# Conditioning as fp32 matmuls on raw weight tiles, and query/key splits placed behind their transposes, in a two-layer hybrid attention/Fourier step

## The chip, the cores and the metric

The kernel runs on one core of a Trainium2 chip. The metric is the device time of one execution in microseconds. Before the change three runs took 1280.7, 1283.64 and 1284.29 us (median 1283.64).

The core has five engines with an instruction queue of their own: TensorE (PE in the profile, its weight loads PEld), VectorE (DVE), ScalarE (ACT), GpSimd (POOL) and SyncE (SP), which here only issues transfers. Each works through its queue in order; semaphores tie the queues together.

## What is computed

Two layers of a backbone with 1024 features, for 1024 latent tokens and 256 context tokens (ten tiles of 128 tokens, tiles 8 and 9 context). All values are fp32. Cut to what matters here:

```python
def ada_mod(cvec, w, b):
    m = jax.nn.silu(cvec) @ w + b            # w: 1024 x 3072
    return jnp.split(m, 3, axis=-1)          # shift, scale, gate

for l in range(2):
    shc, scc, gtc = ada_mod(c_ctx, ada_w[l], ada_b[l])     # context tokens
    shl, scl, gtl = ada_mod(c, ada_w[l], ada_b[l])         # latent tokens
    hc = modulate(rms_norm(xc, norm_g[l]), shc, scc)       # h * (1 + scale) + shift
    hl = modulate(rms_norm(xl, norm_g[l]), shl, scl)
    yc, yl = mixer(l, hc, hl)      # l=0: attention A and B, gated; l=1: Fourier mixing, gated
    xc, xl = xc + gtc * yc, xl + gtl * yl

# attention A: 8 query heads, 2 key/value heads of width 64
qa = rope(rms_norm(qa, gq)); ka = rope(rms_norm(ka, gk))
p = softmax((qa * 64 ** -0.5) @ concat(ka, ka_ctx).T); oa = p @ concat(va, va_ctx)
# attention B: window of +-128 tokens plus all context keys, and a sink logit per head
```

The conditioning is thus a product of two vectors (c and c_ctx) with two matrices of 1024 x 3072: six parts of 4 MB, named (layer, part) with part 0 the shift, 1 the scale, 2 the gate. Each part is read in eight tiles of 512 KB.

## The kernel before

**Precision.** TensorE multiplies fp32r operands in one pass. To get near fp32, a value is split into a high half (rounded to fp32r) and a low half (the rest), by `copy` for the high half (L261 on ACT, L263 on DVE) and a subtract for the low one (L267 or L641). A product of two such values then takes three matmuls.

**The order of the work.** The program is written in the order of its stages, and a scheduler turns that into one order for each engine. SBUF is cut by hand into pools of equal buffers (`ZONES`: 26 `u`, 8 `w`, 2 `q`, 3 `pt`, 4 `p`, 9 `h`, 4 `e`); `take` gives the longest-free buffer among the pools named, in program order, so a transfer into a buffer waits until its last reader is done. PSUM's banks are three rings: `s` and `t` of three, `a` and `g` of one.

**Opening.** Over eight chunks k of 128 features, `ada_chunk` computes shift and scale of layer 0 for that chunk and the projections of the first tokens follow. A raw tile (128x8x128: eight blocks of 128 rows, 128 columns) is split into halves, and multiplied with `cs4` (the SiLU of the two vectors in both halves, four columns) as the stationary operand: eight matmuls for the high half (L491, four result rows), eight for the low half (L493, two). The rows go to SBUF (L496), and a matmul with `comb` (L499) adds the halves and turns the result into columns, from which `modb` and `moda` are made (L503, L504).

**S1.** A list of steps (`S1`) written by hand: cached keys (`c`), statistics and modulation of the second and third token groups (`n`, `m`), and keys and queries of attention A (`k`, `q`, `K`, `Q`). Each projection returns a function `post`, its finishing; `Filler.run` holds it back until `depth` later steps have been issued (1 in S1). In `q_pair` and `kv_pair` the projected, normalised and rotated queries and keys are split into halves of 128x256 each (`split_v`: `copy` L263 and L641), side by side as `[hi lo]`; `post` transposes the 128-column pieces as fp32r (`transp`, L646), evicts them (`kev`, `qev`) and stores queries to DRAM in `qd` (L762). Before a block of scores `load_q` reads them back (L845) into the `q` pool.

**Attention A.** For each key/value head, ten query tiles (`soft` and the `sL`, `sC` scores at L840, transposes of the probabilities L957, the products with values L963). Between these, work of a `Filler` is pumped in by cost: the remaining projections, by the names in `ORDER` (qa1, kb0, qb0, qb1, f1, g0, ...). With three of them (`COND` = qb0, qb1, g0) go the parts (0, 2), (1, 0) and (1, 1) of the conditioning, by the class `Rows`: in `step_ap` each of the eight tiles (128 rows x 1024) is loaded on SP (L348), multiplied and added to an accumulator for the first vector by two DVE instructions (L351), scaled for the second on ACT (L355) and added on POOL (L356). `finish` then sums the accumulators over the 128 partitions by matmuls with `ones2` (L365, eight of 512 columns, after a split), and turns the rows into columns by eight transposes (`row_to_mod`, L309) or, for a gate, stores them to DRAM in `gtd`.

**Layer 1.** The last part (1, 2), `r2`, stands in the stage of the gate projection (`g1E`, `g1O`, `g1c`, in four chunks): `Rows.step` with four DVE instructions a tile (L339), spread over the last three chunks, and `finish` behind the fourth. Behind that come row sums (L1427, L1429) for the Fourier mixer's first matmuls (`u`).

Of the kernel before, what the change touches and what calls it, by code (L numbers as in the profile page):

```python
# [17 lines left out]
P = 128  # L18
# [12 lines left out]
S1 = "c1 n2 m1 c0 m2 K0 Q0 Q2 K2 k6 q8 k4 k8".split()  # L31
E_ML = ("p", "d")
E_MF, E_MH, LC0 = "da", "d", "ppd"
E_AH, E_AL = "a", "dpp"
# [11 lines left out]
FC, XF = 1.3, False  # L46
AT_C, WO1 = (1, 1), ((0, 1, 2, 3), (), (4,), (5, 6), (7,))
# [4 lines left out]
COND = ("qb0", "qb1", "g0")  # L52
# [70 lines left out]
def hybrid_step(ctx: ExitStack, tc: tile.TileContext, I, O):  # L123
# [44 lines left out]
    qd = dr.tile([NT, 4, 2, 64, 512], F32, name="qd")  # L168
# [26 lines left out]
    cs4 = cp.tile([P, 8, 4], F32R, name="cs4")  # L195
    comb = cp.tile([4, 2], F32, name="comb")
    bT1 = cp.tile([P, 8], F32, name="bT1")
    gT = cp.tile([P, 2, 8], F32, name="gT")
    bT = cp.tile([P, 2, 16], F32, name="bT")
# [17 lines left out]
    dve.tensor_copy(cs4[:, :, 0:2], cs)  # L217
    dve.tensor_sub(cs4[:, :, 2:4], cs, cs4[:, :, 0:2])
    dve.tensor_add(comb, ident[0:4, 0:2], ident[0:4, 2:4])
# [86 lines left out]
    def row_to_mod(l, part, row):  # L306
        tp = t_bank(f"modt{l}{part}")
        for k in range(8):
            pe.transpose(tp[:, 2 * k : 2 * k + 2], row[0:2, k * P : k * P + P], ident[0:2, 0:2])  # L309
        tv = tp[:, 0:16].rearrange("p (k v) -> p k v", v=2)  # L310
# [3 lines left out]
        else:  # L314
# [4 lines left out]
    def ada_src(l, part, k):  # L319
        return I["ada_w"][l, k * P : (k + 1) * P, part * D : (part + 1) * D]  # L320

    class Rows:
        def __init__(self, l, part, name, tags):
            self.l, self.part, self.name, self.tags = l, part, name, tags
            self.acc = [take(tags, (P, D)) for v in range(2)]
            for a in self.acc:
                pool.memset(a.a, 0.0)
                if part == 2:
                    sp.dma_start(a[0:1, :], I["ada_b"][l : l + 1, 2 * D : 3 * D])

        def step(self, k, wt=None):
            own = wt is None
            if own:
                wt = take(self.tags, (P, D))
                sp.dma_start(wt.a, ada_src(self.l, self.part, k))
            for v in range(2):
                for h in range(2):
                    sl = slice(h * 512, h * 512 + 512)
                    dve.scalar_tensor_tensor(  # L339
# [1489 lines left out]
```

## Time and profile before

| what | value |
|---|---|
| runs | 1280.7, 1283.64, 1284.29 us (median 1283.64) |
| the profiled execution's own time | 1282.65 us |
| its span (first to last instruction) | 1280.9 us |
| mean granted TensorE clock | 0.971 |
| busy: PE, DVE, ACT, POOL | 1191.8, 955.5, 639.3, 489.1 us |
| opening | 0 to about 88 us |
| S1 up to the first scores | 88 to 141 us |
| attention A | 141 to about 560 us |
| gate projection of layer 1 | about 1000 to 1075 us |

How to read the quoted lines. A line of a group reads: line of the kernel, engine, operation, result <- operands, tile sizes, count | busy us, mean ns of one | idle time of that engine just ahead of them and what ended it. A line of the waits: the waiting engine, line and tile <- what ended the wait: total us, times, longest us. A line of the chain or the timeline begins with its start and its length in us; the length of a group of matmuls runs to the end of its last one, and ends are modelled, so the distance between two starts is the better price. A matmul on fp32 operands leaves two records (the 16 `comb` matmuls leave 32).

### The profile page before, as it was taken

To read this page: it belongs to the slowest core of one execution; us is meant where nothing else is said; L and a number is where in the kernel's file an instruction comes from. 1 tells how busy PE (TensorE), PEld (TensorE's weight loads), DVE (VectorE), ACT (ScalarE), POOL (GpSimd) and SP (SyncE) were. 2 spreads that over 40 slices of the span, in tenths; PEclk is the share of its full clock that TensorE was granted. 3 is DMA by queue.
4 is the path that set the end of the run, shared out by engine and by line. 5 is a ranking of instruction groups with operands and counts; after the bars stand their busy time and mean duration, and the time that the engine had idled before them with its cause. 6 is when DMAs were issued, how large, how long until landed. Compare 5 with 4: busy or idle time off the path is not lost.

```text
span 1280.9 us, 21997 instructions
## 1 busy us (share of the span) xinstructions
PE 1191.8 (93%) x7883; PEld 1066.0 (83%) x7883; DVE 955.5 (75%) x2114; ACT 639.3 (50%) x1239; POOL 489.1 (38%) x386
## 2 busy tenths in 40 slices
PE   5789899999889899999999978889999998999997
PEld 5788899999879798889999977767777888988886
DVE  6789788776987987977887867466874988548553
ACT  5363366565675576756655677431264324333221
POOL 6757665522775754530101042310411215335001
PEclk8898899999999999999999989889999999999999
DMA  9900332324634336344433388596412544346321
GB/s 303 290 6 31 110 90 71 98 68 107 188 110 134 103 122 177 112 138 129 105 90 87 95 241 223 135 253 202 138 59 75 158 154 142 101 140 191 124 90 66
DMA packets 156199, 168.29 MB, mean 131 GB/s; under 512 B 21917, under 2 KB 117161, under 8 KB 156090
## 3 DMA queue, kind: packets, MB, share of 16 engines
q1 hardware_dynamic: 156090, 166.89, 44.4%
q8 instruction: 62, 1.02, 0.4%
q14 instruction: 47, 0.39, 0.1%
HBM read 122.67 MB, written 44.18 MB: 130 GB/s over the span
## 4 chain that ended last, share of the span: by engine, by line
PE 62%; DVE 15%; DMA 11%; issue 5%; POOL 4%; ACT 3%; SPq 1%; POOLq 0%; DVEq 0%; ACTq 0%
PE ga L249 7%; PE of L249 7%; PE av L963 7%; PE pt L957 6%; PE oz L249 5%; PE q L249 4%; PE u L249 4%; PE g1E L249 4%; PE sL L840 3%; PE g1O L249 2%; DVE w L351 2%; PE kv L249 2%; PE sC L840 2%; DVE p L874 2%; DMA od<-e 2%
## 5 line engine op out<-in xcount | busy, mean ns | idle before, releaser
L960 DVE TENSOR_TENSOR pt<-pt,pt 128x512 fp32r<-128x512 f32 (+1 forms) x264 | 171.1, 658 | 34.5 <-ACT pt L261 34.1
L963 PE MATMUL av<-pt,u 128*128 128x256 f32 x1008 | 171.0, 292 | 7.4 <-DVE pt L960 4.0
L261 ACT ACTIVATE pt<-pt 128x512 fp32r<-128x512 f32 (+1 forms) x264 | 146.9, 574 | 60.8 <-PE pt L957 36.4
L957 PE MATMUL pt<-identr,p 128*128 128x128 f32 x1008 | 156.6, 274 | 0.7 <-ACT h L261 0.5
L963 PEld LDWEIGHTS av<-pt,u 128*128 128x128 f32 x1008 | 142.0, 192 | 16.6 <-DVE pt L960 7.1
L267 POOL TENSOR_TENSOR w<-h,w 128x512 fp32r<-128x512 f32 x58 | 79.6, 1384 | 180.6 <-ACT w L261 78.7
L249 PE MATMUL q<-w,u 128*128 128x256 f32 x864 | 132.3, 294 | 1.8 <-DVE u L438 1.0
L957 PEld LDWEIGHTS pt<-identr,p 128*128 128x128 f32 x1008 | 119.7, 141 | 9.5 <-ACT h L261 0.9
L249 PE MATMUL ga<-u,w 128*128 128x512 f32 (+1 forms) x576 | 123.5, 360 | 0.1
L881 ACT ACTIVATE p<-p,nm 128x1280 f32<-128x1280 f32 (+1 forms) x80 | 95.3, 1192 | 54.7 <-DVE p L874 54.3
L249 PEld LDWEIGHTS q<-w,u 128*128 128x128 f32 x864 | 117.1, 195 | 6.1 <-DVE u L438 1.8
L249 PEld LDWEIGHTS ga<-u,w 128*128 128x128 f32 x576 | 93.7, 188 | 15.0 <-ACT pt L261 0.6
L840 PE MATMUL sL<-u,q 128*128 128x512 f32 x256 | 85.2, 418 | 11.6 <-DVE p L874 8.5
L249 PE MATMUL oz<-u,w 128*128 128x512 f32 x240 | 68.5, 413 | 9.8 <-ACT w L261 9.8
L356 POOL TENSOR_TENSOR w<-w,w 128x1024 f32<-128x1024 f32 x24 | 58.6, 2442 | 43.9 <-ACT w L355 33.4
L881 ACT ACTIVATE p<-p,NM 128x640 f32<-128x640 f32 (+2 forms) x80 | 59.2, 740 | 32.4 <-DVE p L874 32.2
L840 PE MATMUL sC<-u,q 128*128 128x256 f32 x320 | 63.2, 300 | 9.4 <-DMA q<-qd 5.8
L249 PE MATMUL of<-u,u 128*128 128x512 f32 (+1 forms) x219 | 65.8, 388 | 0.0
L249 PEld LDWEIGHTS oz<-u,w 128*128 128x128 f32 x240 | 45.9, 196 | 20.0 <-ACT w L261 10.4
L874 DVE TENSOR_SCALAR_CACHE_REDUCE p<-sC,nsink 128x256 f32<-128x256 f32 x80 | 37.8, 475 | 30.3 <-PE sC L840 25.6
L840 PEld LDWEIGHTS sC<-u,q 128*128 128x128 f32 x320 | 48.9, 192 | 13.4 <-issue 5.8
L249 PE MATMUL kv<-w,u 128*128 128x256 f32 x384 | 56.2, 290 | 0.0
(773 smaller groups left out, 2881.8 us busy)
## 6 DMA issues: line engine op xcount, KB each, us to landing
q<-qd SPq DMA_DIRECT2D x80, 256.0 KB
w<-i_ada_w SPq DMA_DIRECT2D x24, 512.0 KB
h<-i_w_in SPq DMA_DIRECT2D x40, 256.0 KB
qd<-h SPq DMA_DIRECT2D x40, 256.0 KB
h<-i_w_out SPq DMA_DIRECT2D x32, 256.0 KB
h<-i_wuT SPq DMA_DIRECT2D x16, 256.0 KB
u<-i_x SPq DMA_DIRECT2D x8, 512.0 KB
p<-i_ada_w SPq DMA_DIRECT2D x8, 512.0 KB
```

The costliest lines, as they stand in the source:

```text
L249: pe.matmul(out, a, b, start=i == 0, stop=i == n - 1)
L261: act.activation(out, in_, AF.Copy)
L267: pick("lo" + lc, lc).tensor_sub(dst_l, src, dst_h)
L351: dve.scalar_tensor_tensor(out=self.acc[0][:, sl], in0=wt[:, sl], scalar=cs[:, k, 0:1], in1=self.acc[0][:, sl], op0=ALU.mult, op1=ALU.add,)
L356: pool.tensor_add(self.acc[1].a, self.acc[1].a, wt.a)
L840: pe.matmul(ps, q[:, s, hc * P : hc * P + P], keys, start=s == 0, stop=s == 1)
L874: dve.tensor_scalar(p[i][:, end[i] : end[i] + n], ps, sign, last[i], op0=ALU.mult, op1=ALU.min, accum_out=c)
L881: act.activation(p[i][:, 0 : end[i]], p[i][:, 0 : end[i]], AF.Exp, bias=last[i], scale=-1.0, accum_out=SU[:, t, hd + i, 0:1],)
L957: pe.transpose(tp[:, jj * 256 + i * P : jj * 256 + i * P + P], p[i][:, off : off + P], ident)
L960: dve.tensor_sub(pt[:, 1, 0:n], tp[:, 0:n], pt[:, 0, 0:n])
L963: pe.matmul(acc, vv, pt[:, s, jj * 256 : jj * 256 + 256], start=c + jj + s == 0, stop=c + jj == nt - 1 and s == 1,)
```

## The change

**Conditioning.** All 48 tiles of the conditioning are now column tiles (128x8x128) that go to TensorE raw: `ada_mm` takes each 128x128 fp32 block as the stationary operand and `cs` (128x2) as the moving one, eight fp32 matmuls a tile, accumulating straight into columns in PSUM. `cs4`, `comb`, the splits, the class `Rows` and `row_to_mod` are gone. The 16 tiles of (0, 0) and (0, 1) stay in the opening. The other 32 are issued in S1 ahead of its steps, in the numbers of `AT_N` (0, 0, 2, 2, 2, 2, 3, 3, 3, 3, 4, 4, 4), into the pools `p`, `pt`, `q`, with the `a` bank for the sum. The gate parts are transposed once at the end of S1 (`gate_rows`) and stored to `gtd`.

**Queries and keys.** They are transposed unsplit as fp32 (four transposes for a pair of query tiles in place of eight, two for a pair of key tiles in place of four) and split when they are taken from PSUM: a `copy` for the high half, a DVE subtract for the low one. The halves of the keys come to lie in separate partitions (`key_split`; `kd` has the high half in one part and the low in the other, loaded in four pieces). Queries are staged in a 4 KB tile from the pools of `QE_Z` in place of two buffers of `h`, and `qd` and the scores' indexing (`q_at`) follow.

**Finishing.** In S1 `depth` is 3 in place of 1.

```diff
+AT_N, AT_Z = (0, 0, 2, 2, 2, 2, 3, 3, 3, 3, 4, 4, 4), ("p", "pt", "q")
+QE_Z = ("pt", "q", "w", "u", "p")
-COND = ("qb0", "qb1", "g0")
...
+    def ada_mm(out, raw, first, last):
+        for b in range(8):
+            pe.matmul(out, raw[:, b, :], cs[:, b, :], start=first and b == 0, stop=last and b == 7)
+        drop(raw)
...
+    def ada_step(l, part, k, raw, tag="g"):
+        if k == 0:
+            acc_ada[l, part] = bank(tag, f"ada{l}{part}")
+        ps = acc_ada[l, part]
+        ada_mm(ps[:, 2 * k : 2 * k + 2], raw, k == 0, k == 7)
+        if k < 7:
+            return
...
+        else:
+            col = take("e", (P, 2, 8))
+            dve.tensor_add(col.a.rearrange("p v k -> p k v"), tv, bb)
+
+            def row_out():
+                tp = t_bank(f"gt{l}")
+                pe.transpose(tp[0:16, 0:P], col.a.rearrange("p v k -> p (v k)"), ident)
+                row = take("e", (16, P))
+                act.activation(row.a, tp[0:16, 0:P], AF.Copy)
+                sp.dma_start(gtd[l].rearrange("v (k c) -> (v k) c", c=P), row.a)
...
     def ada_chunk(k, raws):
         ps = bank("g", f"ada{k}")
         for part, raw in enumerate(raws):
-            hi, lo = take("u", (P, 8, P), F32R), take("u", (P, 8, P), F32R)
-            split(hi.a, lo.a, raw.a, E_AH, E_AL)
-            drop(raw)
-            out = ps[0:4, part * P : part * P + P]
-            for b in range(8):
-                pe.matmul(out, cs4[:, b, :], hi[:, b, :], start=b == 0, stop=False)
-            for b in range(8):
-                pe.matmul(out[0:2], cs4[:, b, 0:2], lo[:, b, :], start=False, stop=b == 7)
-            drop(hi, lo)
...
+            ada_mm(ps[:, 2 * part : 2 * part + 2], raw, part == 0, part == 1)
...
+    def transp(name, y, n):
+        tp = t_bank(name)
         for i in range(n):
-            pe.transpose(tp[:, i * P : i * P + P], y2[:, i, :], identr)
+            pe.transpose(tp[:, i * P : i * P + P], y[:, i, :], ident)
         return tp
+    def key_split(dst, tp, h):
+        a, b = 64 * h, 64 - 64 * h
+        copy("kev", E_KEV, dst[a : a + 64], tp[a : a + 64])
+        dve.tensor_sub(dst[b : b + 64], tp[a : a + 64], dst[a : a + 64])
...
         def post():
+            tp = transp(f"qT{m}{kv}{t}", y.rearrange("p t (a h) d -> p (t a) (h d)", h=2), 4)
+            tv = tp.rearrange("p (t n) -> p t n", t=2)
+            qe = take(QE_Z, (P, 2, 2, 256), F32R)
+            copy("qev", E_QEV, qe[:, :, 0, :], tv)
+            dve.tensor_sub(qe[:, :, 1, :], tv, qe[:, :, 0, :])
             for i in range(2):
-                tp = transp(f"qT{m}{kv}{t}{i}", y2[i].a, 4)
-                qe = take("h", (P, 512))
-                copy("qev", E_QEV, qe.a, tp)
-                sp.dma_start(qd[t + i, 2 * m + kv].rearrange("a d f -> (a d) f"), qe.a)
+                sp.dma_start(qd[t + i, 2 * m + kv], qe[:, i].rearrange("p a n -> p (a n)").bitcast(F32))
...
     fl_ = Filler()
-    fl_.depth = 1
+    fl_.depth = 3
...
+    todo_ada = deque((l, part, k) for l, part in ((0, 2), (1, 0), (1, 1), (1, 2)) for k in range(8))
+    def ada_fill(n):
+        for _ in range(min(n, len(todo_ada))):
+            l, part, k = todo_ada.popleft()
+            ada_step(l, part, k, ada_tile(l, part, k, AT_Z), "a")
     for n, op in enumerate(S1):
+        ada_fill(AT_N[n])
...
-        if nm in cond:
-            for n in range(4):
-                cost, fn, key = (*work[n], None)[:3]
-                fl_.add(0.5 * cost, fn, key)
-                fl_.add(0.0, cond_steps(cond[nm], (2 * n,)))
-                fl_.add(0.5 * cost, cond_steps(cond[nm], (2 * n + 1,)))
...
-    r2 = Rows(1, 2, "ad12", BIG)
-        for k in ((), (0, 1, 2), (3, 4, 5), (6, 7))[c]:
-            r2.step(k)
-    r2.finish("g")
```

**How the order moves.** In these rows stand a row's number on its engine, the line of the kernel, the operation, the result <- operands by the program's names, and the size with its count.

First TensorE in S1. The change has four blocks of this kind (here the first, at row 360; the others at 387, 408 and 509), in which the eight tiles of one part follow each other; `q` are projections of queries, `kT` a transpose of keys:

```order
359 L244 MATMUL q_1371<-w_376,u_992 128x256
360 L313 MATMUL ada_813<-cs,p_811 128x2 x8
361 L313 MATMUL ada_813<-cs,pt_822 128x2 x8
362 L313 MATMUL ada_813<-cs,q_912 128x2 x8
363 L313 MATMUL ada_813<-cs,p_922 128x2 x8
364 L313 MATMUL ada_813<-cs,pt_942 128x2 x8
365 L313 MATMUL ada_813<-cs,q_952 128x2 x8
366 L313 MATMUL ada_813<-cs,p_1022 128x2 x8
367 L313 MATMUL ada_813<-cs,p_1032 128x2 x8
368 L583 MATMUL kT_1322<-identr,q_1046 128x128 x2
369 L244 MATMUL q_1371<-w_375,u_993 128x256
```

Before, no conditioning stands between the opening and the first scores (`sL`), of which this is the place:

```order
611 L249 MATMUL q_1828<-w_438,u_1110 128x256
612 L249 MATMUL q_1828<-w_439,u_1110 128x256
613 L249 MATMUL q_1828<-w_438,u_1111 128x256
614 L646 MATMUL kT_1686<-identr,p_1562 128x128 x4
615 L840 MATMUL sL_0000_1708<-u_1019,q_1701 128x512 x2
616 L249 MATMUL q_2001<-w_428,u_1050 128x256
```

All four blocks stand ahead of the first scores, which are row 573 in the change; after the last conditioning tile of the opening (row 212) come 77 matmuls of projections before the next transposes of x.

Second SP's queue around that place, in the change: raw tiles (`i_ada_w`) into the pools `p`, `pt` and `q`, stores of queries (`qd<-`), then the first loads of queries (`q<-qd`):

```order
91 L308 DMA q_1457<-i_ada_w 128x8x128
92 L308 DMA pt_1467<-i_ada_w 128x8x128
93 L710 DMA qd<-p_1563 128x512 x2
94 L308 DMA p_1568<-i_ada_w 128x8x128
95 L308 DMA p_1578<-i_ada_w 128x8x128
96 L308 DMA pt_1588<-i_ada_w 128x8x128
97 L807 DMA q_1750<-qd 64x2x512 x2
98 L807 DMA q_1946<-qd 64x2x512 x2
```

Before, the queue holds only the stores, weights and loads there:

```order
65 L762 DMA qd<-h_1414 128x512
66 L282 DMA h_1672<-i_w_in 128x2x256
67 L282 DMA h_1668<-i_w_in 128x2x256
68 L845 DMA q_1701<-qd 64x2x512
69 L704 DMA o_new_v_a<-h_1625 128x128 x2
70 L762 DMA qd<-h_1655 128x512
```

The 32 raw tiles of S1 are rows 59 to 96 of SP's queue; the two loads of queries stand behind all of them. Later, in attention A, the staging tiles of the queries lie in the `q` pool for most pairs, between the loads that use its two buffers.

Third TensorE at the passage from the gate projection (`g1c`) to the Fourier mixer (`u`), before:

```order
5056 L249 MATMUL g1c_12675<-u_11710,u_12261 128x256
5057 L249 MATMUL g1c_12675<-u_11709,w_12262 128x256
5058 L365 MATMUL ad12p_12710<-h_12711,ones_88 2x512
5059 L365 MATMUL ad12p_12710<-h_12712,ones_88 2x512
5060 L365 MATMUL ad12p_12710<-h_12717,ones_88 2x512
5061 L249 MATMUL u_12857<-u_12753,u_11468 128x258
```

and in the change:

```order
5008 L244 MATMUL g1c_12174<-u_11262,u_11790 128x256
5009 L244 MATMUL g1c_12174<-u_11263,u_11790 128x256
5010 L244 MATMUL g1c_12174<-u_11262,q_11791 128x256
5011 L244 MATMUL u_12294<-w_12222,u_11021 128x258
5012 L244 MATMUL u_12294<-u_12223,u_11021 128x258
```

The `ad12p` rows between the two are gone. On DVE the row sums (L1368 and L1370 in the change) now begin at row 1375, ahead of the last projection chunk's finishing; before, their counterparts (L1427, L1429) stand partly among the `Rows` steps and partly behind them.

More of the change, by code (lines that the diff above doesn't have):

```diff
@@ L474, in ada_load @@
     def ada_load(k):
-        out = []
-        for part in range(2):
-            raw = take(("p", "pt", "q"), (P, 8, P))
-            c0 = part * D + k * P
-            sp.dma_start(raw.a, I["ada_w"][0, :, c0 : c0 + P].rearrange("(b p) c -> p b c", p=P))
-            out.append(raw)
-        return out
+        return [ada_tile(0, part, k, ("p", "pt", "q")) for part in range(2)]
     def ada_chunk(k, raws):
@@ L827, in hybrid_step @@
     drop_w(wka)
+    for fn in gate_rows:
+        fn()
     ws["qa1"] = load_w(w0cols(C_QA + 256))
```

189 lines of the change are left out of this document (56 added, 133 removed).

## The prediction

> **What bounds the kernel now.** I read the page first: its totals, the 40 slices and the shares of the chain that ended last.
>
> ```profile
> span 1280.9 us, 21997 instructions
> PE 1191.8 (93%) x7883; PEld 1066.0 (83%) x7883; DVE 955.5 (75%) x2114; ACT 639.3 (50%) x1239; POOL 489.1 (38%) x386
> DMA  9900332324634336344433388596412544346321
> PE 62%; DVE 15%; DMA 11%; issue 5%; POOL 4%; ACT 3%; SPq 1%; POOLq 0%; DVEq 0%; ACTq 0%
> ```
>
> TensorE is busy 93% of the span, but only 62% of the chain is its own; DVE, POOL, ACT and transfers hold a quarter. So an edit that gives TensorE more to do can be free in some stages and full price in others, and the sum has to go by stages. The view of busy time in windows, cut where the stages change:
>
> ```profile
> 40.00:64.00 24.00, 20.54 (x163) 19.41 (x164) 17.05 (x18) 9.01 (x12) 17.63 (x9) 0.78 0.94 296
> 64.00:88.00 24.00, 24.00 (x236) 23.55 (x235) 18.84 (x32) 16.46 (x29) 12.81 (x11) 0.95 0.03 7
> 88.00:141.00 53.00, 42.49 (x311) 39.98 (x308) 47.55 (x110) 18.24 (x39) 41.21 (x37) 0.87 0.24 72
> 157.00:316.00 159.00, 159.00 (x1270) 152.61 (x1269) 123.92 (x313) 97.35 (x166) 72.04 (x77) 1.00 0.30 84
> 316.00:560.00 244.00, 225.97 (x1650) 204.09 (x1649) 210.90 (x436) 156.31 (x261) 148.09 (x103) 1.00 0.48 141
> 1075.00:1177.00 102.00, 98.11 (x714) 89.44 (x713) 69.92 (x134) 36.84 (x88) 51.38 (x42) 0.98 0.49 151
> ```
>
> Columns: length, then busy time of TensorE, its weight loads, DVE, ACT, POOL, the granted clock, the DMA share and GB/s. The opening is bound by transfers to 64 us (share 0.94); then nothing is left to load (0.03), yet the first layer's conditioning runs on to 80. From 88 to 141 DVE (47.6 of 53) and POOL (41.2) set the pace and TensorE idles 10.5 us. From 157 on attention A is all TensorE; but from 316 to 560, where the `Rows` steps are fed in, 18.0 us of TensorE idle appear, at 211 us of DVE. What ends that idle time, and what the `Rows` steps cost there, by the view of waits from 316 to 560 and the groups:
>
> ```profile
> PE sL L840 <- DVE p L874: 8.5, 7, 1.6
> PE av L963 <- DVE pt L960: 3.8, 5, 1.3
> PE sC L840 <- DVE p L874: 2.7, 2, 2.0
> ```
>
> ```profile
> L351 DVE SCALAR_TENSOR_TENSOR w<-w,cs,w 128x512 f32<-128x512 f32 x48 | 52.6, 1134 | 4.7 <-DMA w<-i_ada_w 3.9 <-DMA w<-i_ada_b 0.6
> L356 POOL TENSOR_TENSOR w<-w,w 128x1024 f32<-128x1024 f32 x24 | 58.6, 2442 | 43.9 <-ACT w L355 33.4 <-issue 8.5 <-DMA w<-i_ada_w 1.9
> ```
>
> 15.0 us of waiting is for the softmax on DVE, which shares its engine with 52.6 us of conditioning. The same softmax between 157 and 316 made TensorE wait for nothing.
>
> **The price of the new matmul.** A raw tile (128x8x128 fp32) now takes eight fp32 matmuls, 128 columns of weights stationary and two columns moving. Before has four instructions of that width (pcol, with one row), in the timeline of TensorE:
>
> ```profile
> 1139.14 0.56 PE L1555 MATMUL pcc<-h,u 128*128 128x256 f32 x3
> 1139.63 0.49 PE L1555 MATMUL pcc<-pt,w 1*128 1x256 f32 x2
> 1140.06 0.62 PE L1555 MATMUL pcc<-h,u 128*128 128x256 f32 x3
> 1140.61 1.05 PE L1600 MATMUL pcol<-identr,h 1*128 1x2 f32 x8
> 1141.59 0.63 PE L1555 MATMUL pcc<-h,u 128*128 128x256 f32 x3
> ```
>
> The four make eight records in 0.98 us (1140.61 to 1141.59): two records each, 0.1225 us a record. One row against 128 should not matter: the 1-row pair in this fence takes 0.215 a record (1139.63 to 1140.06), the 128-row triples 0.163 and 0.183. Lower bound, twelve fp32 transposes with 128-column stationaries, from the chain:
>
> ```profile
> 278.61 1.31 PE pt L957 x12
> 279.92 2.15 PE kv L249 x18
> ```
>
> That is 0.109. I take 0.115 a record, 1.84 us a tile (1.74 to 1.96). The Trainium skill (TensorE: Matmul & The Clock Gate, section "LDWEIGHTS (loading the stationary operand)") gives P/1.2 ns for P columns, whatever the rows: 107 ns for 128, an estimate of 1.71 a tile, just under my lower row.
>
> **Opening, 0 to 88.** Per pair of tiles this goes:
>
> ```profile
> 74.80 0.60 PE L499 MATMUL modt<-comb,e 4*128 4x2 f32 x4
> 75.33 0.64 PE L491 MATMUL ada<-u,cs 128*4 128x128 f32 x8
> 75.81 0.64 PE L493 MATMUL ada<-u,cs 128*2 128x128 f32 x8
> ...
> 77.24 0.69 PE L510 MATMUL kv0s<-w,u 128*128 128x256 f32 x4
> ```
>
> Sixteen matmuls at 0.060 for a tile (75.33 to 75.81 for eight) and two `comb` records at 0.13: 1.2 us, against 1.84 now, so TensorE has 16 x 0.6 = 10 us more. But the splits (16 on ACT, 16 on DVE and POOL), the row's eviction and the hop through `comb` go, and a tile can be consumed as it lands. After the last tile the order leaves some 77 projection matmuls, at 0.12 each (18 in 2.15 us above): 64 + 1.8 + 9.2 = 75 at best; the bound above is 88, nothing gained. DVE's 18.8 busy in that window is mostly row statistics, which stay, so I take 80: **-8** (-14 to 0).
>
> **S1, 88 to 141.** The other 32 tiles come here in four blocks of eight: 32 x 1.84 = **+59** (55.8 to 62.7). What hides it is TensorE's idle time: 10.5 by the records, more by the starts, since a record's end is modelled and runs into the next (311 at 0.12 are 37 of the 53: 16 idle). I take all of it, **-16** (0 to -16), since the blocks depend on transfers alone. If that cover fails, all 59 count. Not the transfers: at 297 GB/s (row above) 32 x 512 KB take 57 us, and 0.24 x 53 = 13 us of others stand there already, 70 in all in a stage that becomes some 97 long. Nor the finishing lag of three: it delays transposes that nothing waits for before the first scores. The first scores (141.0 before) should start at 141 - 8 + 59 - 16 = 176.
>
> **Transposes of queries and keys.** 208 fp32r ones become 108 fp32 ones:
>
> ```profile
> 323.61 0.45 PE L646 MATMUL kT<-identr,h 128*128 128x128 f32 x4
> 323.89 0.48 PE L840 MATMUL sC<-u,q 128*128 128x256 f32 x2
> ```
>
> 0.07 each against 0.109: 108 x 0.109 - 208 x 0.07 = **-3**. The splits ahead of them took POOL this (from the groups), and now become 34 DVE subtracts behind them:
>
> ```profile
> L641 POOL TENSOR_TENSOR h<-h,h 128x256 fp32r<-128x256 f32 x46 | 35.4, 786 | 18.3 <-DVE h L263 16.5 <-PE kT L646 0.7 <-DMA qd<-h 0.6
> L263 DVE CAST h<-h 128x256 fp32r<-128x256 f32 x47 | 21.2, 485 | 7.0 <-POOL h L671 2.7 <-ACT h L743 2.4 <-ACT h L691 1.7
> ```
>
> DVE also loses the casts of the second row, so its balance is about even (34 at 0.6, the cost of a 128x512 pass at most, against 21.2): nothing. If DVE still set the pace, some 20 us of subtracts would count in part, and that lies inside the bounds of the next part.
>
> **316 to 560 (qb0, qb1, g0).** Out of TensorE go 24 `ones2` matmuls and the 16 row transposes:
>
> ```profile
> L365 PE MATMUL ad02p<-h,ones 128*2 128x512 f32 x8 | 2.8, 404 | 0.0
> L309 PE MATMUL modt<-identr,w 2*128 2x2 f32 x16 | 1.6, 202 | 0.0
> 1041.52 5.55 PE g1E L249 x24
> ```
>
> 24 x 0.231 (a 512-column matmul, third row) + 16 x 0.1 = **-7**. The idle time goes too if the `Rows` load made it: 18.0 by records, some 26 with the records counted by their pitches; I take **-21** (0 to -26), between the two.
>
> **r2, 1000 to 1087.** Its 32 DVE steps (20 of them in the first row below, at 0.81), eight `ones2` matmuls and the stores behind them go. The group, and the chain there:
>
> ```profile
> L339 DVE SCALAR_TENSOR_TENSOR u<-u,cs,u 128x512 f32<-128x512 f32 x20 | 15.3, 814 | 2.8 <-DMA u<-i_ada_w 2.8
> ```
>
> ```profile
> 1069.94 4.64 DMA g1d<-u
> ...
> 1077.30 5.66 DVE u L1429 x9
> ...
> 1086.78 13.33 PE u L249 x97
> ```
>
> The row sums L1429 stand behind the `Rows` steps on DVE; now they run before the last projection chunk, and TensorE goes straight from g1c to u. 8 x 0.231 = 2 plus the 4 us idle from 1075 to 1177 and about one more: **-7** (-2 to -11).
>
> **The q pool.** The split queries are staged in any of five pools, and in attention A mostly in the two buffers of `q`, from which the scores read. A load can then wait for a store:
>
> ```profile
> 737.23 3.70 DMA q<-qd
> ```
>
> Five blocks' loads are affected, with 4.5 to 8 us of matmuls in front by the order: **+1** (0 to +8).
>
> Sum: -8 + 59 - 16 - 3 - 7 - 21 - 7 + 1 = **-2** on the span. The profiled execution's own time is 1282.65 (span 1280.9), 1 below the runs' median 1283.64: 1282.65 - 2 = **1281**, rounded up.
>
> **Rivals.**
> - **More cover.** The opening ends at 75 (-5), 26 instead of 21 go in 316 to 560 (-5), r2 gives 11 (-4) and the records come at 0.109 (-3): 1264, or half of that, 1273. For it: 157 to 316 runs without idle time at 124 of 159 on DVE, and after the change every stage up to 560 is as lightly loaded. Against: the statistics in the opening stay.
> - **The idle time in 316 to 560 stays (slower).** The waits are for L874, the softmax's reduction. If its own latency makes them, and not what is queued ahead of it on DVE, taking `Rows` away gives none or half of the 21 back: 1291 to 1302. It decides as soon as more than 7 remain. For it: L874 is named as the releaser, `Rows` nowhere. Against: the same softmax before 316 made no wait.
> - **The q pool.** If each of the five loads shows its whole 3.7 us: +17 at most, some +8 in the middle: 1286 to 1298.
> - **Dearer fp32.** If a full-height weight takes four passes with a load each where the one-row pcol took two, a tile is 3.7 us: 48 x 1.84 = 88 more: 1369. The Trainium skill (FP8 and Floating Point Precision, section "TensorE Precision Notes") says that true FP32 makes four passes through the array; pcol and `comb` show two records an instruction, so the four either lie inside the two or are not made.
> - That the tiles don't land where the table puts them is excluded by the order: all 32 stand ahead of the first scores.
>
> **How the numbers follow.** A kernel of this length can be told from no change beyond 0.3%, 3.9 us: faster is under 1279.8, slower over 1287.5. Forecast (1274 to 1288) 0.47, of which 0.20 faster, 0.23 same, 0.04 slower; more cover 0.21, faster; idle stays 0.17, slower; q pool 0.11, 0.04 of it same; dearer fp32 0.04. Together faster 0.41, same 0.27, slower 0.32. As the cases have both signs, the range goes from 1263 to 1299; the likeliest case alone is 1274 to 1288.
>
> **What would show it.** The pitch of the `ada` records at 0.109 to 0.123; the first sL at about 176 (170 with a short opening, 186 or more without cover); conditioning of layer 0 over by about 68 and the opening by 80; PE waits for L874 after the first scores of qb0 to g0 at most a few us in all, where they were 11; a straight passage from g1c to u; waits of sL for q<-qd under 2 us. The forecast is wrong if S1 grows by more than 45 us or by less than 28, or if the idle time of 316 to 560 returns behind another engine.

## The result, and the profile after

The changed kernel takes 1365.9 us (median of four runs, 1364.39 to 1369.03); the kernel before 1282.17 in the runs beside them. The ratio is 1.0655, with a 95% interval from 1.0627 to 1.0683. The forecast was 1281, in a range from 1263 to 1299. Nearest to the time came the rival that had 0.04, "dearer fp32" with 1369; its reason turned out to be wrong all the same, as shown below.

The page of the profile after:

```profile
span 1362.7 us, 22266 instructions
PE 1301.3 (95%) x8217; PEld 1185.2 (87%) x8217; DVE 834.9 (61%) x1993; ACT 581.9 (43%) x1161; POOL 330.8 (24%) x281
PEclk8676555899999999999999998997999999998999
PE ada L313 9%; PE of L244 8%; PE ga L244 8%; PE av L925 7%; PE q L244 7%; PE pt L919 6%; PE oz L244 5%; PE sL L802 4%; PE kv L244 4%; PE g1E L244 3%; PE g1O L244 3%; PE u L244 3%; PE sC L802 2%; DMA h<-i_w_in 2%; PE g1c L244 2%
```

The row of the granted TensorE clock on the page before:

```profile
PEclk8898899999999999999999989889999999999999
```

DVE, ACT and POOL have less to do, as the change says: DVE is busy 835 us where it was 955, POOL 331 where it was 489. But the new matmuls (`ada`) lead the chain with 9%, and the row of the granted clock, which was 8 or 9 tenths in every slice before, reads 6, 7, 6, 5, 5, 5 from the second to the seventh. The windows of the opening, of S1 and of attention A, with the clock in the third column from the right:

```profile
40.00:60.00 20.00, 20.00 (x109) 20.00 (x110) 7.77 (x19) 6.00 (x10) 2.28 (x2) 0.59 1.00 291
120.00:140.00 20.00, 20.00 (x95) 20.00 (x96) 13.49 (x31) 1.17 (x3) 12.31 (x10) 0.50 0.52 147
140.00:160.00 20.00, 20.00 (x111) 20.00 (x110) 0.00 (x0) 0.00 (x0) 0.00 (x0) 0.59 0.60 169
245.00:270.00 25.00, 19.88 (x133) 17.64 (x132) 19.74 (x49) 10.23 (x18) 15.18 (x13) 0.86 0.26 79
420.00:664.00 244.00, 241.10 (x1791) 226.62 (x1790) 169.31 (x422) 136.48 (x253) 55.55 (x47) 1.00 0.35 100
```

In the two windows of S1 TensorE has no idle time (20.00 of 20), and yet the granted clock is 0.50 and 0.59. From 140 to 160 DVE, ACT and POOL do nothing at all. Just behind the first scores, from 245 to 270, TensorE idles 5.1 us. In attention A from 420 on the clock is full, and the idle time is 2.9 us in 244, where it was 18.0. One block of S1 tile by tile, in the timeline of TensorE:

```profile
113.29 2.24 PE L313 MATMUL ada<-cs,p 128*128 128x2 f32 x16
115.39 1.93 PE L313 MATMUL ada<-cs,pt 128*128 128x2 f32 x16
117.18 3.24 PE L313 MATMUL ada<-cs,q 128*128 128x2 f32 x16
120.29 3.55 PE L313 MATMUL ada<-cs,p 128*128 128x2 f32 x16
123.70 3.55 PE L313 MATMUL ada<-cs,pt 128*128 128x2 f32 x16
```

The first tile takes 2.10 us from start to start, the second 1.79 (0.112 a record, the price that was forecast), the third 3.11, the fourth and later ones 3.41 (0.213 a record). The price doubles, to that of half the clock. So it isn't that a full-height weight costs more: it is the clock that goes. It goes 4.2 us after the start of this block, and 3.3, 2.8 and 2.2 us after the starts of the others. In the trace's record of the granted clock only 0.50 and 1.00 occur (0.59 is a mixture of the two), in stretches of whole multiples of 3.41 us, and the four falls, at 117.5, 144.8, 172.2 and 209.7, lie 8, 8 and 11 times 3.41 us apart. So how long a block keeps the full clock depends here on where in this grid it begins. The four blocks in the chain:

```profile
113.49 24.00 PE ada L313 x128
...
141.73 24.15 PE ada L313 x128
...
169.52 24.59 PE ada L313 x128
...
207.69 25.16 PE ada L313 x128
```

97.9 us for 32 tiles, against 59. The matmuls of the three milestones by which the stages can be compared (last projection of the opening, first and last local scores), after and before, first and last start in the middle of the row:

```profile
L447 PE MATMUL q2s<-w,u x48: 279/415/561, 44.3 to 95.9; 128*128 128x256 f32 x48
L802 PE MATMUL sL<-u,q x256: 387/396/795, 241.7 to 636.8; 128*128 128x512 f32 x128
```

```profile
L510 PE MATMUL q2s<-w,u x48: 276/280/415, 46.2 to 87.7; 128*128 128x256 f32 x48
L840 PE MATMUL sL<-u,q x256: 388/397/503, 141.0 to 550.3; 128*128 128x512 f32 x128
```

| stage | before | after | measured | forecast |
|---|---|---|---|---|
| opening, to the last q2s | 87.7 | 95.9 | +8.2 | -8 |
| S1, from there to the first sL | 53.3 | 145.8 | +92.5 | +43 |
| first sL to the end of the span | 1139.9 | 1121.0 | -18.9 | -37 |
| span | 1280.9 | 1362.7 | +81.8 | -2 |

How much of this the clock can make, by an estimate: with half of every stretch at half clock counted as lost, a mean granted clock of 0.971 in 1280.9 us loses 37 us, and one of 0.923 in 1362.7 us loses 105. The difference is 68 of the 82 us.

### The profile page after: what moved, and what is told of

The parts are those of the page before. It is cut to its first block, busy times and chain, and to the rows that moved or that the text cites. A ratio compares the mean times of both kernels' runs of the same rounds, so it can differ in the third digit from the quotient of the medians.

```text
span 1362.7 us, 22266 instructions
## 1 busy us (share of the span) xinstructions
PE 1301.3 (95%) x8217; PEld 1185.2 (87%) x8217; DVE 834.9 (61%) x1993; ACT 581.9 (43%) x1161; POOL 330.8 (24%) x281
## 4 chain that ended last, share of the span: by engine, by line
PE 77%; DMA 10%; DVE 5%; issue 3%; SPq 2%; ACT 2%; POOL 1%; POOLq 0%; DVEq 0%; ACTq 0%
PE ada L313 9%; PE of L244 8%; PE ga L244 8%; PE av L925 7%; PE q L244 7%; PE pt L919 6%; PE oz L244 5%; PE sL L802 4%; PE kv L244 4%; PE g1E L244 3%; PE g1O L244 3%; PE u L244 3%; PE sC L802 2%; DMA h<-i_w_in 2%; PE g1c L244 2%
## 5 line engine op out<-in xcount | busy, mean ns | idle before, releaser
L262 POOL TENSOR_TENSOR w<-h,w 128x512 fp32r<-128x512 f32 x61 | 82.5, 1369 | 252.7 <-DVE w L258 110.7
L244 PE MATMUL q<-w,u 128*128 128x256 f32 x864 | 136.5, 295 | 1.7 <-DVE u L397 1.7
L802 PE MATMUL sC<-u,q 128*128 128x256 f32 x320 | 60.8, 295 | 4.0 <-DMA q<-qd 1.8
L313 PEld LDWEIGHTS ada<-cs,p 128*128 128x128 f32 x352 | 63.5, 281 | 0.1
L313 PE MATMUL ada<-cs,p 128*128 128x2 f32 x352 | 63.3, 313 | 0.0
L244 PE MATMUL kv<-w,u 128*128 128x256 f32 x384 | 59.0, 301 | 0.0
L244 PE MATMUL of<-u,u 128*128 128x512 f32 (+1 forms) x173 | 55.5, 387 | 0.0
```

What stands on the lines that cost most here:

```text
L244: pe.matmul(out, a, b, start=i == 0, stop=i == n - 1)
L262: pick("lo" + lc, lc).tensor_sub(dst_l, src, dst_h)
L313: pe.matmul(out, raw[:, b, :], cs[:, b, :], start=first and b == 0, stop=last and b == 7)
L802: pe.matmul(ps, q_at(q, s, hc), keys, start=s == 0, stop=s == 1)
```

## The experiments

Two theories stood at the start. Theory A: the clock follows how many columns stream through the array, and an fp32 matmul that loads 128 columns of weights to stream two counts as near idleness. Theory B: the clock falls for what full-height fp32 weights draw. Besides, S1's blocks could have cost by their place alone, and a part of the loss could belong to queries and keys.

**More work for TensorE: eight filler matmuls a tile.**

```diff
             pe.matmul(out, raw[:, b, :], cs[:, b, :], ...)
+            pe.matmul(pad, identr, wide, start=False, stop=...)   # pad: ps[:, 128:512]; wide: identity, three times, 384 columns
```

> The changed kernel with one matmul more behind each of its 384 fp32 matmuls: fp32r, 384 columns of the identity moving, into unused columns of the same PSUM bank (0.17 us each at full clock by the pitch of a 512-column one, 66 us in all); nothing is left out. Theory A (the clock follows how many columns stream through the array; an fp32 matmul with two moving columns counts as nearly idle): the granted clock in the conditioning blocks rises from 0.50 to about 1.0, a tile takes 1.75 + 1.4 = 3.1 us in place of 3.4, and the time falls to 1345 to 1365 although TensorE is given 66 us more. Theory B (the clock falls for what full-height fp32 weights draw): the clock stays at 0.5 or below, a tile takes 3.4 + 2.8 = 6.2 us, the time rises to about 1366 + 48 x 2.8 = 1500, at least 1440.

Measured: 1366.82 us, ratio 1.0636 (1.0601 to 1.0670): the same time as the change, with 384 matmuls more, and just above theory A's range. The page's row of the clock, and windows of S1:

```profile
PEclk9798999899999999999999999898999899998999
```

```profile
120.00:140.00 20.00, 20.00 (x153) 20.00 (x151) 7.84 (x23) 1.01 (x2) 7.46 (x8) 1.00 0.50 141
140.00:160.00 20.00, 20.00 (x155) 19.99 (x154) 6.14 (x13) 0.76 (x2) 5.36 (x3) 1.00 0.64 180
```

The clock is 1.00 where it was 0.50 and 0.59, and an fp32 matmul with its filler takes 0.40 us:

```profile
121.32 0.42 PE L315 MATMUL ada<-identr 128*128 128x384 f32 x1
121.58 0.28 PE L313 MATMUL ada<-cs,p 128*128 128x2 f32 x2
121.72 0.42 PE L315 MATMUL ada<-identr 128*128 128x384 f32 x1
```

3.2 us a tile, filler and all, is less than the 3.41 without. Theory B falls: more work raised the clock. That the whole time didn't fall as theory A had it: S1 is 10 us shorter than in the change (135.3 from the last `q2s` to the first `sL`), but the opening is 6 longer (102.1, at a clock of 0.72 from 40 to 60), and the rest behind the first scores 7 longer, for which no run here gives the reason.

**Fewer fillers.** Two and four a tile (behind every fourth, and every second, fp32 matmul), all else as in the run above.

> The changed kernel with two further matmuls of 384 columns for each conditioning tile (behind the fourth and the eighth fp32 matmul; 96 in all, some 0.2 us each, 19 us), where the run before had eight. Theory A (clock by streamed columns): if that is still enough activity, the clock in the blocks is near 1.0, a tile takes about 2.2 us in place of 3.4 and the time is 1305 to 1320; if it isn't, 0.5 to 0.6, a tile of about 4.1 us, 1385 to 1400. Either way it places the point from which the clock is kept. Were it not the clock but the eight-fold filler that hid something else, 1366 + 19 = 1385.

Measured: 1392.19 us, ratio 1.0837 (1.0799 to 1.0875), in the range for a clock that isn't kept (0.50 from 140 to 160).

> The changed kernel with four filler matmuls of 384 columns a tile, between the run with eight (clock 1.0 in S1) and that with two (0.5). Theory A (clock by streamed columns over a stretch of a few us): the switch lies between, so either 1.0 and about 2.5 us a tile (about 1330) or 0.5 and 4.8 us (about 1430).

Measured: 1391.95 us in one run, without an interval, near neither of the two forecasts: the opening kept most of its clock (0.91 from 40 to 60, where the change had 0.59), S1 didn't (0.50 to 0.67 from 120 to 220). A window of the run with four, and the point at which its clock goes, in the timeline:

```profile
140.00:160.00 20.00, 20.00 (x101) 19.93 (x101) 1.03 (x3) 0.76 (x2) 0.00 (x0) 0.59 0.46 132
```

```profile
146.78 0.50 PE L313 MATMUL ada<-cs,p 128*128 128x2 f32 x4
147.14 0.42 PE L315 MATMUL ada<-identr 128*128 128x384 f32 x1
147.40 0.50 PE L313 MATMUL ada<-cs,pt 128*128 128x2 f32 x4
147.76 0.52 PE L315 MATMUL ada<-identr 128*128 128x384 f32 x1
148.08 0.85 PE L313 MATMUL ada<-cs,pt 128*128 128x2 f32 x4
148.78 0.67 PE L315 MATMUL ada<-identr 128*128 128x384 f32 x1
```

At full clock 384 columns came in every 0.62 us here (146.78 to 147.40), and it wasn't enough: at 148 the step grows to 1.17. With eight fillers it was 384 in 0.40 us, and it was. So with these fillers the point lies between some 620 and 960 streamed columns per microsecond. It isn't a bare count of columns, though: in the change itself, from 96.8 to 103.6, TensorE ran 33 records, all fp32 transposes of 128 columns, with 2 us of idle time. That is at most 620 columns per microsecond too, and the clock was 1.00 there and up to 107. Those columns stream more slowly (0.109 us for 128, against 0.231 for 512 in a projection, by the rows of the forecast). So the share of time in which columns stream would fit both, and the runs don't test it.

**The same products with the operands exchanged.** `cs` becomes the stationary operand (two columns), the raw block the moving one (128 columns); the two result rows are evicted by ACT and turned by a small transpose; S1's sums use bank g.

```diff
-            pe.matmul(out, raw[:, b, :], cs[:, b, :], start=first and b == 0, stop=last and b == 7)
+            pe.matmul(rows, cs[:, b, :], raw[:, b, :], start=b == 0, stop=b == 7)
         drop(raw)
+        row = take("e", (2, P))
+        act.activation(row.a, rows, AF.Copy)
+        pe.transpose(out, row.a, ident[0:2, 0:2])
```

> The changed kernel with the operands of the conditioning matmuls exchanged: cs (two columns) stationary, the raw 128x128 fp32 block moving, eight a tile into two rows of PSUM, which ACT evicts and one small transpose a tile turns into columns; bank g in place of a in S1. The weights loaded are two columns, the streamed ones 128. Theory A: the clock stays near 1.0 in the opening's and S1's tiles. Theory B' (any fp32 matmul on this data lowers the clock): 0.5 as in the change. The price of a record isn't known (no row has fp32 with 128 moving columns and few weights): 0.06 to 0.22, 1 to 3.5 us a tile; at 1.8 the time is 1300 to 1320, at 3.5 about 1370.

Measured: 1299.48 us, ratio 1.0115 (1.0071 to 1.0159): 66 us less than the change, at the lower edge of what theory A had for 1.8 us a tile. A window and two tiles of it:

```profile
140.00:160.00 20.00, 17.18 (x143) 13.48 (x142) 3.55 (x13) 3.66 (x10) 0.00 (x0) 1.00 0.57 165
```

```profile
41.36 1.91 PE L313 MATMUL ada<-pt,cs 128*2 128x128 f32 x16
43.20 0.74 PE L456 MATMUL kv0s<-w,u 128*128 128x256 f32 x4
...
146.40 1.91 PE L313 MATMUL ada<-p,cs 128*2 128x128 f32 x16
148.72 0.22 PE L317 MATMUL adat<-identr,e 2*128 2x2 f32 x1 [0.42 <-ACT e L316]
148.87 1.91 PE L313 MATMUL ada<-pt,cs 128*2 128x128 f32 x16
```

Sixteen records in 1.84 us: the price at full clock is that of the prediction, 0.115 a record, for either placing of the operands. With 128 columns in 0.115 us, 1100 columns stream per microsecond, or 830 with the wait behind the tile counted in (2048 in the 2.47 us from 146.40 to 148.87), and the clock stays at 1.00. This run moves S1's sums to bank g as well; what that gives by itself follows below.

**Exchanged, and without its waits.** In the run above each tile in S1 waits 0.42 us for ACT (last fence). Here two tiles share an eviction, their transposes come one pair later, and gate rows are stored as rows:

```diff
+        if k % 2 == 0:
+            return
+        row = take("e", (2, 256))
+        act.activation(row.a, acc_ada["ps"][0:2, 0:256], AF.Copy)
+        while gate_rows:
+            gate_rows.pop(0)()        # transposes of the pair before
```

> The run with exchanged operands again, without its 18 us of waits in S1: there each of 32 tiles was followed by 0.42 us of TensorE waiting for ACT's eviction and a transpose. Here two tiles share an eviction, their transposes come one pair later, and gate rows go to DRAM without any. If price and clock were the whole error of the prediction, this is the change as it was costed (1.84 us a tile at full clock): 1299 - 18 = 1281, ratio 0.995 to 1.002. If the other terms were too high as well (S1's cover, the idle time after the first scores), 1288 to 1299.

Measured: 1290.93 us, ratio 1.0042 (1.0013 to 1.0072), in the second range: the price and the clock were not the whole error. That is the change as it was costed, with the clock kept but for single stretches, and it lies some 10 us above the forecast. The scores in it, and the last tiles in the chain:

```profile
L461 PE MATMUL q2s<-w,u x48: 276/280/288, 41.7 to 84.6; 128*128 128x256 f32 x48
L816 PE MATMUL sL<-u,q x256: 387/396/502, 166.5 to 572.8; 128*128 128x512 f32 x128
```

```profile
166.49 0.71 PE sL L816 x2
167.64 5.26 PE ada L314 x32
173.35 3.66 PE ada L314 x32
```

Here four of S1's 32 tiles (64 records) run after the first scores, and 26 records before the last projection of the opening. With these set back into S1 at 0.115 a record (7.4 and 3.0 us), the opening has -6.1 (forecast -8), S1 +39.0 (forecast +43) and the rest -22.3 (forecast -37). By this account price and cover in S1 were about right, and the remaining error lies behind the first scores.

**Tiles one at a time in attention A.** The change with S1's 32 tiles spread among the projections and scores:

```diff
-        ada_fill(AT_N[n])
...
+        if nm in cond:      # qb0, qb1, g0, g1
+            for n in range(4):
+                cost, fn, key = (*work[n], None)[:3]
+                fl_.add(0.4 * cost, fn, key)
+                fl_.add(0.3 * cost, one_step(cond[nm], 2 * n))
+                fl_.add(0.3 * cost, one_step(cond[nm], 2 * n + 1))
...
```

> The changed kernel with the 32 tiles of S1 moved into attention A, one tile at a time between projections and scores (with qb0, qb1, g0, g1, the first three being where Rows stood before). Theory A: a tile of 1.8 us alone between dense matmuls doesn't lower the clock: granted clock 0.97 or more in attention A, 0.11 us a record, 32 x 1.8 = 57 us more in attention A and about 100 less in S1: 1310 to 1330. Theory B: the clock falls around each tile, 0.2 us a record: 1350 or more. If the slowness were the blocks keeping DVE waiting and not the clock, S1 would lose some 40 us and attention A win no more than 57: about 1340 to 1366.

Measured: 1341.03 us, ratio 1.0435 (1.0376 to 1.0494), above the range of theory A and at the lower end of the one that makes DVE's waiting the cause. Between dense matmuls a tile runs at the full price, as theory A said:

```profile
337.69 1.84 PE L313 MATMUL ada<-cs,w 128*128 128x2 f32 x16
339.40 0.72 PE L825 MATMUL sC<-u,q 128*128 128x256 f32 x4
```

```profile
580.00:670.00 90.00, 85.00 (x502) 78.59 (x501) 41.02 (x131) 33.76 (x79) 8.04 (x7) 0.83 0.50 137
```

16 records in 1.71 us are 0.107 each, and the clock is 0.97 and 0.99 from 330 to 580. S1 is 60.8 us long, 85 less than in the change, where waiting for DVE alone would have given 40; so the third reading falls. What was too low is the sum: S1 lost 85 and not 100, and behind the first scores the tiles cost 67 and not 57. Where the last of them lie (580 to 670) the clock is 0.83 and TensorE idles 5 us. The blocks alone, in another bank:

```diff
-            ada_step(l, part, k, ada_tile(l, part, k, AT_Z), "a")
+            ada_step(l, part, k, ada_tile(l, part, k, AT_Z), "g")
```

> The changed kernel with S1's conditioning sums in PSUM bank g in place of a, which the unfinished queries of tiles 2 and 3 hold until late in S1. By the order the tiles of (0, 2) then come early, in ones and twos between projections and transposes, and (1, 0) to (1, 2) in blocks as before. Theory A: the scattered tiles run at a higher clock (0.12 to 0.16 a record), and 5 to 10 us of idle time in S1 is filled: 1335 to 1355. If position and cover don't matter and the price is the tile's own, no change: 1362 to 1369.

Measured: 1352.55 us, ratio 1.0528 (1.0482 to 1.0575), within the first range: scattering one of four blocks among projections gives back 13 us by the times, 16 by the ratios. It isn't told apart here how much of that is the clock and how much is cover.

**The two halves of the change apart.** The conditioning alone, on the kernel before (the hunks on `ada_*`, S1, `Rows`; queries, keys and lag as before):

> The kernel before with the conditioning of the change alone (queries and keys as before, lag 1). If the loss is all of the conditioning's, this is as slow as the changed kernel or slower by the transposes' 3 us: 1362 to 1372. If a part of it comes from queries and keys (q pool, the subtracts on DVE), it lies lower by that part.

Measured: 1368.43 us, ratio 1.0648 (1.0613 to 1.0683), against 1.0655 for the whole change. The loss is the conditioning's, all of it.

Queries and keys alone (`transp`, `key_split`, `q_at`, `qe`, `load_q`, `kd`, `qd`):

> The kernel before with the queries' and keys' splits behind their transposes alone (conditioning as before, lag 1). By the prediction's terms -3 for the transposes and +1 for the q pool: 1278 to 1282, ratio 0.996 to 1.000. If the subtracts on DVE compete with Rows there, up to 20 us more: 1285 to 1300.

Measured: 1289.20 us (median of ten), ratio 1.0059 (1.0029 to 1.0090): slower by some 7 us where -2 was the forecast. Waits of TensorE in attention A in this run, and in the kernel before:

```profile
PE sL L856 <- DMA q<-qd: 15.3, 8, 3.9
```

```profile
PE sL L840 <- DMA q<-qd: 2.7, 2, 2.2
```

The waits for query loads go from 2.7 to 15.3 us: the mechanism of the rival on the q pool. Its price isn't shown. The profiled execution is the shortest of the ten (1282.47 us), no longer than that of the kernel before: its local scores take 12.5 us longer from first to last (421.8 against 409.3), and what follows them is 11.8 shorter. So the 7 us of the median can't be put down to these waits. In the whole change they don't show (1.9 us in attention A). To see whether the pool is the cause, its staging tiles were kept out of it:

```diff
-QE_Z = ("pt", "q", "w", "u", "p")
+QE_Z = ("pt", "w", "u", "p")
```

> The kernel before with the queries' and keys' splits behind their transposes, as in the run of that part alone, but with the staging tiles kept out of pool q. If the shared q pool made the 15 us of TensorE's waits for q<-qd seen there, these fall to about 3 as in the kernel before, and the time lies 8 to 12 below that run: ratio 0.990 to 0.998 to before. If other work (subtracts on DVE) takes the place of the waits, no change: 1.003 to 1.009.

Measured: 1299.48 us, ratio 1.0104 (1.0072 to 1.0137), above both ranges. The waits for `q<-qd` are gone from the list, so the pool did make them; but the time didn't fall. Others have come in their place:

```profile
PE av L979 <- DVE pt L976: 9.4, 7, 3.7
PE sL L856 <- DVE p L890: 6.0, 5, 2.2
```

Here a wait that was removed was replaced by others, mostly behind DVE. That the load of `Rows` makes these is likely, since with `Rows` gone the part costs nothing that can be measured, but no run tests it.

**What is worth keeping.** The opening alone with exchanged operands, everything else as before:

```diff
-            split(hi.a, lo.a, raw.a, E_AH, E_AL)
...
-                pe.matmul(out, cs4[:, b, :], hi[:, b, :], start=b == 0, stop=False)
...
+            pe.matmul(out, cs[:, b, :], raw[:, b, :], start=b == 0, stop=b == 7)
```

> The kernel before with one part alone changed: the 16 tiles of the opening as raw fp32 moving operands with cs stationary (no splits, no comb), all else as before. In the run with exchanged operands the opening's projections ended at 83.3 in place of 87.7: so -4, ratio 0.994 to 0.999. If the following stage (88 to 141, paced by DVE and POOL) takes it back: 1.000.

Measured: 1280.39 us, ratio 0.9954 (0.9924 to 0.9985): this beats both kernels, by 4 to 6 us against the one before. The opening's last projections, the first scores, and a window:

```profile
L506 PE MATMUL q2s<-w,u x48: 276/281/286, 38.2 to 78.8; 128*128 128x256 f32 x48
L836 PE MATMUL sL<-u,q x256: 387/397/628, 134.0 to 542.5; 128*128 128x512 f32 x128
```

```profile
40.00:64.00 24.00, 24.00 (x203) 19.98 (x201) 7.08 (x21) 8.22 (x15) 2.37 (x3) 1.00 1.05 307
```

It ends at 78.8 in place of 87.7, the first scores come 7.0 earlier, and of this 2.7 are left at the end of the span in the profiled executions. The window from 40 to 64 ran at 0.78 before, now at 1.00.

The same with (0, 2) in S1 in place of one of the three `Rows`:

> As the run on the opening alone, and the eight tiles of (0, 2) with exchanged operands in S1 in place of one of the three Rows: 8 x 1.84 = 15 us of TensorE where the kernel before has 10 to 16 us idle, and a third of Rows (17 us of DVE, 20 of POOL) less in attention A. If the cover in S1 is real: 6 to 8 us of attention A's idle time go at a cost of 0 to 5, with the opening 1272 to 1280, ratio 0.991 to 0.998. If S1's idle time can't be filled: 1283 to 1292.

Measured: 1282.52 us, ratio 0.9999 (0.9971 to 1.0027), between the two ranges. S1's idle time could be filled: the first scores come at 137.4, 3.4 later than in the run before this one, for 14.7 us of tiles. But nothing of it is left at the end; in the profiled execution the local scores take 413.6 us from first to last, where the run before had 408.5.

## Why the prediction was wrong

**The step that failed** is the price of the new matmul: "I take 0.115 a record, 1.84 us a tile (1.74 to 1.96)". The number is right for a tile by itself: 1.79 in the second tile of a block, 0.107 between dense matmuls, 1.84 with the operands exchanged. What the step left out is that the price is one at the granted clock, and that a run of such matmuls lowers the clock: in the blocks a tile cost 3.41, all 32 took 97.9 us where 59 had been summed, and S1 grew by 92.5 where more than 45 was the sign of being wrong. The rows it was taken from, four instructions of pcol between dense ones (0.98 us), were too short to show it. The run of twelve transposes stood for the lower bound, but each of those streams 128 columns. A clue was in a quoted row and wasn't used: the window from 40 to 64 had a clock of 0.78 with TensorE busy 20.5 of 24. What lowered it there isn't shown.

With the operands exchanged and the waits removed, which keeps the clock (and, through bank g, S1's cover), the ratio goes from 1.0655 to 1.0042: 79 of the 84 us by which the change is slower. Bank g by itself gives 13 to 16; how much of that is again the clock isn't told apart.

Point by point:
- **What bounds the kernel** held: attention A is all TensorE, and the idle time from 316 to 560 was the load of `Rows` on DVE. It fell from 18.0 to 2.9 us in a window of the same length (1.2 in the run of the conditioning alone), and L874's successor has left the list of waits. The slower rival on this fell.
- **Opening.** -8 is about what the opening gives at full clock: 78.8 against 87.7 in the run of it alone, 84.6 in the whole change with exchanged operands, 3.0 of it for tiles of S1. In the change it was +8.2, at a clock of 0.59 to 0.68 from 20 to 88.
- **S1.** +59 was 97.9 for the blocks, by the clock. The cover of 16 held with exchanged operands and bank g (+39.0 for +59 - 16), but not in the change: without its blocks S1 took 47.9 us there, 5.4 less than the 53.3 before. Its sums wait in bank a, which the early queries hold, so the tiles come as blocks, in which the other engines have little to do (0.00 from 140 to 160), and TensorE idles before the first (4.5 us from 96 to 113) and after the last (5.1 from 245 to 270).
- **Transposes of queries and keys.** -3, with nothing for the subtracts, and +1 for the q pool. Alone this part is slower by 0.6%, for which the runs don't show the reason; with `Rows` gone it makes no difference that can be measured (1.0648 without, 1.0655 with).
- **316 to 560.** -28 in all (7 and 21), in attention A as a whole: 409.3 us from the first local score to the last became 395.1, and 398.9 with exchanged operands (406.3 less 7.4 for the tiles there). Some 10 to 14, then: the term was two to nearly three times what came. The terms were taken from one window, and new idle time stands at the start of attention A, from 245 to 270 (4.6 of the 5.1 us is one wait of a key transpose for POOL).
- **r2.** -7 came out in its own stage: from the first gate projection to the last u it took 191.7 us (943.4 to 1135.1) and takes 185.5 (1026.2 to 1211.7). TensorE worked on other rows of u during most of the chain's 17 us between g1c and u; a piece of the chain that isn't TensorE's is not idle time of TensorE, and the forecast rightly counted only the idle part. But the stretch behind the last u, which the change leaves as it was, took it back. Before and after:

```profile
1135.10:1162.00 26.90, 26.90 (x195) 21.81 (x193) 20.04 (x37) 12.13 (x25) 15.57 (x11) 1.00 0.69 220
1211.70:1244.50 32.80, 32.80 (x196) 27.06 (x194) 20.54 (x39) 12.50 (x25) 16.41 (x12) 0.79 0.57 180
```

The same matmuls, with TensorE busy throughout, take 5.9 us more, at a clock of 0.79 in place of 1.00. The runs of the opening and of queries and keys alone have 27.0 and 27.1 us there, that of the conditioning alone 32.9. The exchanged change without its waits has 32.9 too in its profiled execution, some 6 of the 10 us by which it missed the forecast.

- **The rivals.** "Dearer fp32" came near the time by chance: its four passes with a load each would have shown in the first two tiles of a block, which took 2.10 and 1.79 us and not 3.7. The Trainium skill (TensorE: Matmul & The Clock Gate, section "What's actually happening") says that activity releases a clock gate that is closed by default, to half of the full rate; the granted clock of 0.50 and 0.213 against 0.107 a record agree with the two rates. Its advice for keeping the clock (same page, section "Why this matters for your kernels") is to leave no idle gaps; here the clock fell with no gap (20.00 of 20 busy), so what counts as activity is not that TensorE is busy by the profile's records.

What stays open: the exact measure by which the clock is set. Fillers and the exchange change both the columns that stream and the share of time in which weights are loaded, and the runs don't tell these two apart. Nor is the point between 620 and 960 columns per microsecond of filler known closer. And why the stretch behind the last u keeps its clock in some runs and not in others isn't shown.

## What to carry to other kernels

A price read from a few instructions holds at the clock of their surroundings: before costing a long run of a new kind of matmul, ask how much of its time columns stream, and quote the granted clock with the price. Where one operand has two columns and the other 128, let the narrow one be the stationary one: here the price of a record was the same and the clock was kept, at the cost of an eviction and a small transpose that have to be kept off TensorE's path. And pieces of a chain that belong to other engines are not idle time of the engine that bounds the kernel; its own busy time in the window says what can be won.

## What the runs showed of the hardware

- Back-to-back fp32 matmuls with 128x128 weights and two moving columns run at 0.107 to 0.115 us a record, two records each, for 2 to 4 us in the four blocks here; then the granted clock falls to 0.50 and a record takes 0.213, with TensorE busy all the time. The falls lie whole multiples of 3.41 us apart.
- 384 more streamed columns for every fp32 matmul (960 columns per microsecond) keep the clock at 1.00 and make a tile cheaper than without (3.2 against 3.41 us); half as many (620) don't keep it. A stretch of fp32 transposes kept it at no more than 620, so the bare number of columns isn't the measure.
- The clock is a property of the stretch, not of the instruction: the 18 projections between two blocks took 3.71 us (0.206 each; 0.12 in attention A), and single tiles between dense matmuls ran at full price.
- One and the same stretch of matmuls, with TensorE busy throughout, took 27 us in some runs (clock 1.00) and 33 in others (0.79).
- An fp32 matmul with two stationary and 128 moving columns costs the same as with 128 and two: 0.115 us a record.
